# Emitting each q and v projection one unit further ahead in a state-space stage

## The chip, the core and the metric

The kernel runs on one core of one Trainium2 chip. The metric is the device time of one execution in microseconds (us), the median over several executions. The five engines are TensorE (PE, with its weight loads shown as PEld), VectorE (DVE), ScalarE (ACT), GpSimd (POOL) and SyncE (SP, here a queue for transfers).

## What is computed

The reference is one layer of a hybrid trunk on 1024 tokens of width 1024. Only its first third is touched by the change:

```
proj = x @ w_in[i]
q, k, v, u = jnp.split(proj, [ATTN_WIDTH, 2 * ATTN_WIDTH, 3 * ATTN_WIDTH], axis=-1)
...
a_out = _diff_attention(q, k, v, lam, lam_init, subln_g[i])
s_out = _s5_mixer(u, ssm_a_re[i], ssm_a_im[i], ssm_log_dt[i], ssm_b_re[i], ssm_b_im[i],
                  ssm_c_re[i], ssm_c_im[i], ssm_d[i], w_glu[i], b_glu[i])
mix = jnp.concatenate([a_out, s_out], axis=-1) @ w_out[i]
h = _layernorm(alpha * x + mix, ln1_g[i], ln1_b[i])
moe = _hier_moe(h.reshape(b_ * s_, d_), ...).reshape(b_, s_, d_)
x = _layernorm(alpha * h + moe, ln2_g[i], ln2_b[i])
```

The input projection gives q, k, v (4 heads of 128 columns each) and u (512 columns). The attention reads q, k and v; the state-space mixer, a diagonal complex recurrence over 32 groups of 16 channels, reads u alone. So the projections of q, v and k owe nothing to the recurrence and can be worked beside it. A mixture of 32 experts follows and takes more than half of the time.

## The kernel before

All sixteen column tiles of 128 of the input projection go through `proj(ct)`: 48 matmuls of 128x512 (line 244, `proj`), three passes of split-precision products over 8 row tiles, into a PSUM pair of banks. There are two such pairs, used in turn, so that the projection after next can begin only when the result of this one has been copied out. The weights of a column tile arrive by one transfer into a single buffer of the area `misc` (line 191) and are split into a high and a low part, half by half, by a cast on ACT and a subtraction on DVE (tiles `wa` and `wb`, lines 174 and 155). Tiles 12 to 15 are u and come first. Tiles 0 to 3 are q (`proj_q`, copied out by ACT at line 668 into `qr`). Tiles 8 to 11 are v (`proj_v`: copied by ACT at line 678, transposed by PE at line 683, copied again by ACT at line 684). Tiles 4 to 7 are k (`proj_k`: two casts on ACT, lines 692 and 693, and two subtractions on DVE, all four reading the PSUM pair).

The state-space mixer goes through eight units of four channel groups. `ssm_prepare(u)` makes the parameters of unit u, mostly on POOL: a tile X that PE multiplies and transposes (`pk`, `pw`, lines 570 and 571), the convolution kernel `Ks`, to which DVE adds a diagonal `Dd` that a small transfer brings (line 577), eight transfers that spread it into `Tm` (line 582), and the phase tables. `ssm_unit(u)` is a chain: PE (`pz`, line 606), DVE (three products and a sum), four scans on DVE (line 616), two copies on ACT (lines 619 and 620), three products on DVE that give `H`, PE (`py`, line 627 from `Tm`, line 628 from `H`), and a gelu on ACT and DVE (lines 632 and 634). Its tiles are shared from unit to unit. After every second unit PE transposes the result (`zt`, line 660) and ACT copies it (line 661).

`ssm_pair(c4, fill)` emits two units; for unit u it emits the parameters of unit u+1, then the chain of unit u, then `fill(u)`, which is one projection. Four projections of k follow all units, and then the attention, whose first scores are `s` at line 780.

The order of emission is not the order of the queues. A scheduler of the framework reorders the instructions by priorities that come from the order of emission, and gives out buffers as it goes. Each engine then works through its own queue strictly in order, and an instruction that waits holds up all that stands behind it. So what a move in the code does must be read from the queues.

Of the kernel before, what the change touches and what calls it, by code (L numbers as in the profile page):

```python
# [114 lines left out]
def tile_kernel(ctx: ExitStack, tc: tile.TileContext, I: dict, out: bass.AP, dbg=None):  # L115
# [15 lines left out]
    def bank(name, which=0):  # L131

        if which == 1:
            turn[0] ^= 1
            which = 2 + turn[0]
        return psum.tile([P, 512], F32, tag=f"bank{which}", name=name, bufs=1 if which else 2)
# [4 lines left out]
    def dump(name, t):  # L141
        if name in dbg:
            SP.dma_start(dbg[name], t)
# [13 lines left out]
    def mul(out_, a, b, eng=V):  # L157
        eng.tensor_tensor(out=out_, in0=a, in1=b, op=ALU.mult)  # L158

    def add(out_, a, b, eng=V):  # L160
        return eng.tensor_tensor(out=out_, in0=a, in1=b, op=ALU.add)  # L161
# [70 lines left out]
    def proj(ct):  # L232

        first = ct == 12
        if first:
            turn_x(0)
        wt = split_w(ct)
        o = bank2(f"proj{ct}")

        def products(kt, halves):  # L240
            h_, l_ = xh[kt // 2][:, kt % 2, :], xl[kt // 2][:, kt % 2, :]
            for n, (w_, x_) in enumerate(((0, h_), (0, l_), (1, h_))):
                for hs in halves:
                    PE.matmul(o[:, hs], wt[kt // 4][:, w_, kt % 4, :], x_[:, hs],  # L244
                              start=(kt == 0 and n == 0), stop=(kt == KT - 1 and n == 2))

        for halves in ((HALVES[0:1], HALVES[1:2]) if first else (HALVES,)):
            if first and halves == HALVES[1:2]:
                turn_x(1)
                sl.put(*xraw)  # L250
            for kt in range(KT):
                products(kt, halves)
        return o
# [284 lines left out]
    def wk(name, shape, bufs=1):  # L538
        return areas[where[name]].get(name, shape[1:], bufs=bufs, parts=shape[0])
# [7 lines left out]
    def ssm_prepare(u):  # L547

        gs = slice(4 * u, 4 * u + 4)

        def power(pw, first):
            return pw[:, first:first + 8, gs].rearrange("p k g -> p g k").unsqueeze(3).broadcast_to([P, 4, 8, 16])

        def per_c(b_):
            return b_[:, gs, :].unsqueeze(2).broadcast_to([P, 4, 8, 16])

        def combine(o, a1, b1_, a2, b2_, op, eng, name):
            t_ = wk(name, [P, 4, 8, 16])
            mul(o, a1, b1_, eng)
            mul(t_, a2, b2_, eng)  # L560
            op(o, o, t_, eng)

        X = wk("X", [P, 4, 8, 16])
        combine(X, per_c(BB1), power(LR, 0), per_c(BB2), power(LI, 0), add, G, "tb")

        pk = bank(f"pk{u}")
        pw = bank(f"pw{u}", 1)
        for g in range(4):
            Xg = X[:, g, :, :].rearrange("p k c -> p (k c)")
            PE.matmul(pk[:, 16 * g:16 * g + 16], Xg, CA[:, 4 * u + g, :], start=True, stop=True)  # L570
            PE.transpose(pw[:, g * P:(g + 1) * P], Xg, ident)
        Wm = wk(f"Wm{u % 2}", [P, 4, P])
        S.copy(Wm, pw)
        Ks = wk("Ks", [P, 64], 2)
        S.copy(Ks, pk[:, 0:64])
        Dd = wk("Dd", [16, 4, 16])
        SP.dma_start(Dd, I["ssm_d"][0, gs].partition_broadcast(16))
        mul(Dd, Dd, ident[0:16, 0:16].unsqueeze(1).broadcast_to([16, 4, 16]))
        add(Ks[0:16, :], Ks[0:16, :], Dd.rearrange("p g c -> p (g c)"))
        Tm = Tms[u % 2]  # L580
        for t_ in range(8):
            SP.dma_start(Tm[16 * (7 - t_):P, t_].rearrange("p g c -> p (g c)"), Ks[0:16 * (t_ + 1), :])
        M = wk(f"M{u % 2}", [P, 4, 8, 16])
        combine(M, per_c(CA), power(LR, 1), per_c(CB), power(LI, 1), add, G, "tb")

        def low(a_):
            return a_[:, gs, :].unsqueeze(2).broadcast_to([P, 4, 8, 16])

        def high(a_):
            return a_[:, gs, :].unsqueeze(3).broadcast_to([P, 4, 8, 16])  # L590


        C = wk(f"C{u % 2}", [P, 4, 8, 16])
        Sn = wk(f"Sn{u % 2}", [P, 4, 8, 16])
        combine(C, low(cL), high(cH), low(sL), high(sH), sub, G, "tb")
        combine(Sn, low(sL), high(cH), low(cL), high(sH), add, V, "tv")
        return Wm, Tm, M, C.rearrange("p g a b -> p g (a b)"), Sn.rearrange("p g a b -> p g (a b)")
# [42 lines left out]
    def ssm_pair(c4, fill):  # L640
        z2 = wk("z2", [P, 8, P])
        if c4 % 2 == 0:
            zT[c4 // 2] = sl.get([P, 2, T], F32, f"zT{c4 // 2}")
        UT = UTs[c4 // 2][:, c4 % 2, :, :]
        for u in (2 * c4, 2 * c4 + 1):
            if u + 1 < NG // 4:
                made[u + 1] = ssm_prepare(u + 1)
            if u + 2 == NG // 4:
                spp.close()
                areas[0].close()  # L650
            ssm_unit(u, UT, z2, made.pop(u))
            if u + 2 == NG // 4:
                areas[1].close()
            fill(u)
        if c4 % 2 == 1:
            sl.put(UTs.pop(c4 // 2))
        for tq in range(2):
            pz = bank(f"zt{c4}{tq}", tq)
            for t_ in range(4):
                PE.transpose(pz[:, t_ * P:(t_ + 1) * P], z2[:, 4 * tq + t_, :], ident)  # L660
            S.mul(zT[c4 // 2][:, c4 % 2, :].rearrange("p (b t) -> p t b", t=8)[:, 4 * tq:4 * tq + 4, :],
                  pz.rearrange("p (t b) -> p t b", t=4), 0.5)

    def proj_q(h):
        o = proj(h)
        if h % 2 == 0:
            qr[h // 2] = sl.get([P, 2, T], F32, f"qr{h // 2}")
        S.mul(qr[h // 2][:, h % 2, :], o, 0.125)
# [27 lines left out]
        kk[h] = t_  # L696

    fills = [(proj_q, 0), (proj_q, 1), (proj_q, 2), (proj_q, 3), (proj_v, 0), (proj_v, 1), (proj_v, 2), (proj_v, 3)]
    made[0] = ssm_prepare(0)
    for c4 in range(4):  # L700
        ssm_pair(c4, lambda u: fills[u][0](fills[u][1]))
    dump("zT0", zT[0])
    dump("zT1", zT[1])
    for a_ in areas[2:5]:
# [182 lines left out]
    fills = {}  # L887
# [729 lines left out]
```

## Time and profile before

| what | value |
| --- | --- |
| median of 3 runs | 1185.71 us (1184.47 to 1189.87) |
| time of the profiled execution | 1182.18 us |
| span of the profiled execution, first to last instruction | 1180.4 us |
| mean granted clock of TensorE | 0.968 of full speed |
| busy share of PE, DVE, ACT, POOL | 92%, 82%, 60%, 30% |

Rows of the profile give a start in us from the beginning of the span, a length in us, the engine, the line and operation, the tile written and the tiles read, and how often it repeats. A bracket at a row's end is the idle time of the engine just before it and what ended that. The granted clock has two levels, 1.0 (2.4 GHz) and 0.5 (1.2 GHz). Names without a number mean any of their kind: `ssm` stands for any tile of the state-space areas.

### The profile page before, as it was taken

The numbers are of one execution on the slowest core, as the hardware profiler recorded it, in microseconds if no ns is written. First come the engines' busy times: TensorE is split into PE (matmuls) and PEld (weight loads), VectorE is DVE, ScalarE is ACT, GpSimd is POOL, SyncE is SP. The second block draws the span as 40 slices with busy tenths as digits, with TensorE's granted clock in tenths as the row PEclk, the third lists the DMA queues.
The fourth block names the chain that finished last, engine by engine and source line by source line (L and its number), as shares of the span: only waits on it lengthen the run. The fifth ranks groups of instructions, "written<-read, shape, count | busy, mean of one in ns | idle before, by whom it ended". The sixth has DMA issues, their size and how long they took to land.

```text
span 1180.4 us, 15229 instructions
## 1 busy us (share of the span) xinstructions
PE 1081.9 (92%) x5345; PEld 902.0 (76%) x5345; DVE 970.2 (82%) x1430; ACT 711.6 (60%) x960; POOL 359.0 (30%) x297
## 2 busy tenths in 40 slices
PE   6979999896779899995999999999999999999983
PEld 4867887686668788884888888888888888888852
DVE  4898666657878874565999999999999999999955
ACT  3312333445656743213888888888888888888832
POOL 1087464422442643341212122122122122121122
PEclk9989999998999999995999999999999999999997
DMA  8531111211181454545699999999999999999582
GB/s 208 138 99 43 55 46 46 59 30 42 32 325 36 159 210 136 196 178 200 238 361 378 383 369 399 383 385 396 381 374 376 377 370 386 395 386 386 172 208 108
DMA packets 90622, 278.90 MB, mean 236 GB/s; under 512 B 29404, under 2 KB 49900, under 8 KB 66096
## 3 DMA queue, kind: packets, MB, share of 16 engines
q1 hardware_dynamic: 78016, 252.78, 57.1%
q0 software_dynamic: 11520, 24.83, 7.7%
q8 instruction: 43, 0.70, 0.2%
q10 hardware_dynamic: 1008, 0.30, 0.1%
q14 instruction: 35, 0.29, 0.1%
HBM read 254.12 MB, written 34.60 MB: 245 GB/s over the span
## 4 chain that ended last, share of the span: by engine, by line
PE 74%; DVE 13%; ACT 5%; DMA 3%; issue 3%; SPq 1%; POOL 1%; ACTq 0%; DVEq 0%; POOLq 0%
PE g L1246 15%; PE u L1246 14%; PE y L1237 14%; PE proj L244 8%; PE mix L1077 7%; PE xT L1207 3%; DMA misc<-in_w_in_dram 2%; ACT p L783 2%; PE glu L733 2%; PE po L818 1%; PE hT L1219 1%; PE x L1449 1%; PE pl L1099 1%; DVE ssmt L158 1%; DVE ssm L158 1%
## 5 line engine op out<-in xcount | busy, mean ns | idle before, releaser
L1146 POOL DMA_INDIRECT moe_dram<-yo,idx x30 | 52.1, 1738 | 425.9 <-DVE yo L164 425.9
L244 PE MATMUL proj<-xh,wa 128*128 128x512 f32 x256 | 75.9, 403 | 1.7 <-ACT ssm L678 1.6
L244 PE MATMUL proj<-xh,wb 128*128 128x512 f32 x256 | 73.9, 400 | 1.6 <-ACT ssm L678 1.6
L1077 PE MATMUL mix<-woh,mx 128*128 128x512 f32 x256 | 74.3, 401 | 0.7 <-ACT p L783 0.7
L1141 POOL DMA_INDIRECT gx<-h_dram,idx x32 | 60.2, 1881 | 22.5 <-DVE WT L161 13.1
L783 ACT ACTIVATE p<-s,nm 128x1024 f32<-128x1024 f32 (+7 forms) x64 | 47.3, 745 | 26.8 <-DVE nm L798 17.0
L244 PEld LDWEIGHTS proj<-xh,wa 128*128 128x128 f32 x256 | 48.6, 193 | 11.8 <-ACT ssm L678 1.8
L244 PEld LDWEIGHTS proj<-xh,wb 128*128 128x128 f32 x256 | 48.0, 191 | 11.4 <-ACT ssm L678 1.8
L1077 PEld LDWEIGHTS mix<-woh,mx 128*128 128x128 f32 x256 | 48.1, 191 | 10.5 <-ACT p L783 1.0
L1253 ACT ACTIVATE yo<-y,WT 128x1024 f32<-128x1024 f32 (+1 forms) x33 | 36.0, 1091 | 24.4 <-PE y L1237 24.4
L780 PE MATMUL s<-kk,qh 128*128 128x512 f32 (+3 forms) x96 | 38.0, 399 | 12.5 <-ACT p L783 12.2
L818 PE MATMUL po<-vv,half 128*128 128x128 f32 x288 | 43.4, 294 | 6.7 <-ACT half L815 6.6
L818 PEld LDWEIGHTS po<-vv,half 128*128 128x128 f32 x288 | 39.2, 205 | 9.9 <-ACT half L815 8.7
L1207 PEld LDWEIGHTS xT<-ident,gx 128*128 128x128 f32 x256 | 36.2, 208 | 9.9 <-DMA gx<-h_dram,idx 5.8
L1207 PE MATMUL xT<-ident,gx 128*128 128x128 f32 x256 | 36.9, 287 | 7.0 <-DMA gx<-h_dram,idx 5.6
L155 DVE TENSOR_TENSOR xe<-xT,xe 128x1024 fp32r<-128x1024 f32 (+1 forms) x33 | 39.2, 1189 | 4.3 <-ACT xe L174 4.3
L244 PE MATMUL proj<-xl,wa 128*128 128x512 f32 x128 | 42.6, 404 | 0.0
L164 DVE SCALAR_TENSOR_TENSOR yo<-gx,first,yo 128x1024 f32<-128x1024 f32 (+1 forms) x33 | 41.3, 1252 | 1.5
L1077 PE MATMUL mix<-wol,mx 128*128 128x512 f32 x128 | 42.2, 398 | 0.0
L244 PE MATMUL proj<-xl,wb 128*128 128x512 f32 x128 | 41.4, 399 | 0.0
L174 ACT CAST xe<-xT 128x1024 fp32r<-128x1024 f32 (+1 forms) x33 | 32.3, 979 | 13.6 <-PE xT L1207 13.6
L164 DVE SCALAR_TENSOR_TENSOR p<-p,rho 128x1024 f32<-128x1024 f32 (+7 forms) x32 | 36.2, 1135 | 1.0 <-DMA moe_dram<-zero 0.3
(864 smaller groups left out, 3546.7 us busy)
## 6 DMA issues: line engine op xcount, KB each, us to landing
misc<-in_w_in_dram SPq DMA_DIRECT2D x16, 512.0 KB, 3.9
moe_dram<-zero SPq DMA_DIRECT2D x4, 2048.0 KB, 13.2
xr<-in_x_dram SPq DMA_DIRECT2D x8, 512.0 KB, 8.5
wo_raw<-in_w_out_dram SPq DMA_DIRECT2D x4, 1024.0 KB, 4.8
xa<-in_x_dram SPq DMA_DIRECT2D x8, 512.0 KB, 3.5
h_dram<-xa SPq DMA_DIRECT2D x8, 512.0 KB, 3.2
mo<-moe_dram SPq DMA_DIRECT2D x8, 512.0 KB, 6.0
mo<-moe_dram POOLq DMA_DIRECT2D x8, 512.0 KB, 13.1
```

Source lines behind the costliest of these rows:

```text
L155: eng.tensor_tensor(out=out_, in0=a, in1=b, op=ALU.subtract)
L164: return V.scalar_tensor_tensor(out=out_, in0=a, scalar=s, in1=b, op0=op0, op1=op1)
L244: PE.matmul(o[:, hs], wt[kt // 4][:, w_, kt % 4, :], x_[:, hs], start=(kt == 0 and n == 0), stop=(kt == KT - 1 and n == 2))
L780: PE.matmul(s_[:, c0:c0 + w], qd[0][:, c, tk], kk[h][:, c, c0:c0 + w], start=True, stop=False)
L783: S.activation(p_[:, c, 0:n], s_[:, 0:n], AF.Exp, bias=nm[:, c:c + 1], accum_out=L[:, j, c:c + 1])
L818: PE.matmul(po[:, j * P:(j + 1) * P], aT[:, k, :], vv[k // 4][:, k % 4, h * P:(h + 1) * P], start=(k == 0), stop=(k == i))
L1077: PE.matmul(o[-(hs.start > 0)][:, hs], mx[:, m_, kt, :], (woh, wol)[w_][kt // 2][:, kt % 2, hs], start=(kt == 0 and n == 0), stop=(kt == K ...
L1141: return G.indirect_dma_start(out=dst, out_offset=None, in_=h_dram[:, :], in_offset=bass.IndirectOffsetOnAxis(ap=ix, axis=0), bounds_check ...
L1146: G.indirect_dma_start(out=moe_dram[:, :], out_offset=bass.IndirectOffsetOnAxis(ap=ix, axis=0), in_=src, in_offset=None, bounds_check=2 * ...
L1207: PE.transpose(b_[:, kt * P:(kt + 1) * P], rows(g_, kt), ident)
L1237: PE.matmul(y[h_], hid[e][:, x_, kt, :], w_[:, k, HALVES[h_]], start=(kt == 0 and n == 0), stop=(kt == 3 and n == 2))
L1246: PE.matmul(o, xT[e][:, x_, kt, :], w_[:, k, :], start=(kt == 0 and n == 0), stop=(kt == KT - 1 and n == 2))
```

## The change

The list of projections is shifted by one: `proj_q(0)` is emitted directly behind the parameters of unit 0, and unit u is followed by the projection that used to follow unit u+1. Behind unit 7 nothing is emitted any more. No instruction is added, removed or resized.

```
     fills = [(proj_q, 0), (proj_q, 1), (proj_q, 2), (proj_q, 3), (proj_v, 0), (proj_v, 1), (proj_v, 2), (proj_v, 3)]
+    fills.append((lambda _: None, 0))
     made[0] = ssm_prepare(0)
+    proj_q(0)
     for c4 in range(4):
-        ssm_pair(c4, lambda u: fills[u][0](fills[u][1]))
+        ssm_pair(c4, lambda u: fills[u + 1][0](fills[u + 1][1]))
```

The queues show it at three places. In their rows a name ends with the unit or column tile and a serial number: `pk1` belongs to the parameters of unit 1, `proj0` to the first tile of q, `proj1` to the second.

First, PE where the units begin. Before, 29 of the 48 matmuls of `proj0` and `pz0` stand ahead of `pk1`:

```order
L244 MATMUL proj0_833<-xl1_84,wa_66 128x512 x2
L244 MATMUL proj0_833<-xh1_80,wa_66 128x512
L606 MATMUL pz0_797<-UT0_282,ssm10_719 128x128 x4
L244 MATMUL proj0_833<-xh1_80,wa_66 128x512
L244 MATMUL proj0_833<-xh2_81,wa_66 128x512 x2
L244 MATMUL proj0_833<-xl2_85,wa_66 128x512 x2
L244 MATMUL proj0_833<-xh2_81,wa_66 128x512
L570 MATMUL pk1_765<-ssmp0_292,ssm00_718 128x16
L571 MATMUL pw1_766<-ident_72,ssm00_718 128x128
```

After, on the same engine at the end of `proj0`:

```order
L244 MATMUL proj0_766<-xh3_82,wa_66 128x512 x2
L570 MATMUL pk1_821<-ssmp0_292,ssm00_718 128x16
L571 MATMUL pw1_822<-ident_72,ssm00_718 128x128
...
L606 MATMUL pz0_853<-UT0_282,ssm10_719 128x128 x4
L244 MATMUL proj1_889<-xh0_79,wb_67 128x512 x2
L244 MATMUL proj1_889<-xl0_83,wb_67 128x512 x2
L244 MATMUL proj1_889<-xh0_79,wb_67 128x512 x3
L627 MATMUL py0_871<-ssm20_720,UT0_282 128x8x16
L244 MATMUL proj1_889<-xh0_79,wb_67 128x512
```

All 48 matmuls of `proj0` now stand ahead of `pk1`, `pz0` stands behind it, and the first product of `py0` comes seven matmuls into `proj1`.

Second, DVE at the same place, as a piece of the difference. The rows `ssm_722<-pz` begin the chain of unit 0, the row with `ident` is the product that reads the diagonal `Dd` of unit 1, and the rows `wa` split the weights of `proj2`:

```order
 L158 TENSOR_TENSOR ssm_718<-ssmp_293 128x512
-L158 TENSOR_TENSOR ssm_722<-pz_797,ssm_719 128x512
-L158 TENSOR_TENSOR ssm_722<-pz_797,ssm_719 64x512 x2
-L155 TENSOR_TENSOR wa<-misc_68,wa 128x512
+L155 TENSOR_TENSOR wa<-misc_68,wa 128x512 x2
+L158 TENSOR_TENSOR ssm_718<-ssm_718,ident 16x64
+L161 TENSOR_TENSOR ssm_718<-ssm_718 16x64
+L158 TENSOR_TENSOR ssm_722<-pz_853,ssm_719 128x512
+L158 TENSOR_TENSOR ssm_722<-pz_853,ssm_719 64x512 x2
 L161 TENSOR_TENSOR ssm_722<-ssm_722 128x512
 L616 SCALAR_TENSOR_TENSOR ssm_720<-mag,ssm_722 128x128 x4
```

The product with the diagonal, which stood behind the scans of unit 0, now stands ahead of the whole chain of unit 0.

Third, PE where the recurrence ends beside the projections of k (`proj5`, `proj6`, `proj7` are the second to fourth). Before, `py6` stands inside `proj5`:

```order
L244 MATMUL proj5_1878<-xh2_81,wb_67 128x512
L628 MATMUL py6_1606<-ssm10_719,ssm20_720 128x8x16
L627 MATMUL py6_1606<-ssm20_720,UT2_584 128x8x16
...
L244 MATMUL proj5_1878<-xh2_81,wb_67 128x512
L244 MATMUL proj5_1878<-xh3_82,wb_67 128x512 x2
L244 MATMUL proj5_1878<-xl3_86,wb_67 128x512 x2
L244 MATMUL proj5_1878<-xh3_82,wb_67 128x512 x4
```

After, it stands four matmuls ahead of the end of `proj6`:

```order
L244 MATMUL proj6_1947<-xh3_82,wa_66 128x512 x4
L628 MATMUL py6_1673<-ssm10_719,ssm20_720 128x8x16
L627 MATMUL py6_1673<-ssm20_720,UT2_584 128x8x16
...
L244 MATMUL proj6_1947<-xl3_86,wa_66 128x512 x2
L244 MATMUL proj6_1947<-xh3_82,wa_66 128x512 x2
L244 MATMUL proj7_2006<-xh0_79,wb_67 128x512 x2
```

And ACT after, behind `py6`; the casts `kk1` read the PSUM pair of `proj5`, which is the pair that `proj7` takes next:

```order
L632 ACTIVATE ssm40_722<-py6_1673 128x512
L692 CAST kk1_1927<-proj5_1878 64x1024
L693 CAST kk1_1927<-proj5_1878 64x1024
L634 ACTIVATE ssm40_722<-ssm40_722 128x512
L619 COPY ssm40_722<-ssm20_720 64x512
```

Before, the casts `kk1` stood behind `py6` too, but 13 matmuls of `proj5` and all 48 of `proj6` lay on PE between `py6` and `proj7`; now 4 do. In the same way `py7` stood behind the first 11 matmuls of `proj7`, 37 ahead of its end; now it stands behind 40, 8 ahead of the end, and the casts of `proj6` (`kk2`) stand behind it on ACT.

## Rows read from the trace of the kernel before

**Rows 1.** Windows: length, busy PE, PEld, DVE, ACT, POOL, granted clock, DMA share, GB/s.

```profile
126.00:199.00 73.00, 72.59 (x396) 61.84 (x395) 44.74 (x70) 25.45 (x41) 36.12 (x29) 1.00 0.17 44
```

**Rows 2.** Timeline of PE, its rows with idle time, 77 to 126 us.

```profile
85.28 0.61 PE L570 MATMUL pk<-ssmp,ssm 128*128 128x16 f32 x2 [7.65 <-POOL ssm L161]
...
99.37 0.49 PE L628 MATMUL py<-ssm,ssm 128*128 128x128 f32 x2 [1.26 <-DVE ssm L155]
...
119.58 0.49 PE L628 MATMUL py<-ssm,ssm 128*128 128x128 f32 x2 [2.88 <-DVE ssm L155]
```

**Rows 3.** Timeline of PE, its rows with idle time, 126 to 264 us.

```profile
199.41 0.66 PE L683 MATMUL v<-ident,ssm 128*128 128x128 f32 x4 [0.68 <-ACT vv L684]
...
201.66 0.73 PE L244 MATMUL proj<-xh,wa 128*128 128x512 f32 x2 [1.59 <-ACT ssm L678]
...
218.40 0.49 PE L627 MATMUL py<-ssm,UT 128*128 128x128 f32 x2 [0.88 <-ACT zT L661]
...
219.31 1.16 PE L606 MATMUL pz<-UT,ssm 128*128 128x128 f32 x8 [0.43 <-ACT ssm L575]
...
221.85 0.66 PE L683 MATMUL v<-ident,ssm 128*128 128x128 f32 x4 [0.94 <-ACT vv L684]
...
224.10 1.07 PE L244 MATMUL proj<-xh,wb 128*128 128x512 f32 x2 [1.59 <-ACT ssm L678]
...
234.98 0.49 PE L628 MATMUL py<-ssm,ssm 128*128 128x128 f32 x2 [0.79 <-DVE ssm L155]
```

**Rows 4.** Windows, columns as in rows 1, where the clock is lower.

```profile
90.00:91.00 1.00, 1.00 (x4) 0.71 (x4) 0.97 (x2) 0.00 (x0) 1.00 (x1) 0.50 0.45 131
224.00:228.00 4.00, 3.90 (x10) 3.09 (x11) 3.94 (x4) 0.04 (x1) 1.86 (x1) 0.57 0.10 21
```

**Rows 5.** The chain that ended last: start, length, what.

```profile
103.32 1.75 DMA ssm<-in_ssm_d_dram
...
121.41 7.51 PE proj L244 x33
```

**Rows 6.** Timelines: PE behind the first hole, SP's transfers of units 0 and 1.

```profile
87.43 1.63 PE L244 MATMUL proj<-xh,wa 128*128 128x512 f32 x3
...
90.28 3.09 SPq L582 DMA_DIRECT2D ssm<-ssm  x5
93.42 0.59 SPq L577 DMA_DIRECT2D ssm<-in_ssm_d_dram  x1
```

**Rows 7.** Timeline of DVE: the scans of units 0, 1 and 6.

```profile
90.13 5.12 DVE L616 TENSOR_TENSOR_SCAN ssm<-mag,ssm 128x128 f32<-128x128 f32 x4
...
113.48 1.37 DVE L616 TENSOR_TENSOR_SCAN ssm<-mag,ssm 128x128 f32<-128x128 f32 x4
...
225.91 5.68 DVE L616 TENSOR_TENSOR_SCAN ssm<-mag,ssm 128x128 f32<-128x128 f32 x4
```

**Rows 8.** Timelines of ACT and DVE: how `proj6` is copied out.

```profile
257.67 0.60 ACT L632 ACTIVATE ssm<-py 128x512 f32<-128x512 f32 x1
...
259.18 1.01 ACT L693 CAST kk<-proj 64x1024 fp32r<-64x1024 f32 x1
...
260.22 2.46 DVE L155 TENSOR_TENSOR kk<-proj,kk 64x1024 fp32r<-64x1024 f32 x2 [1.23 <-ACT kk L693]
```

**Rows 9.** Timelines of PE, DVE and ACT where the attention begins.

```profile
263.98 0.39 PE L780 MATMUL s<-kk,qh 128*128 128x512 f32 x1
...
265.29 1.22 DVE L798 TENSOR_REDUCE nm<-s 128x1 f32<-128x1024 f32 x1
...
268.04 1.08 ACT L783 ACTIVATE p<-s,nm 128x1024 f32<-128x1024 f32 x1
...
269.26 0.79 PE L780 MATMUL s<-kk,qh 128*128 128x512 f32 x1 [3.33 <-ACT p L783]
```

**Rows 10.** Timelines of DVE and PE in unit 2: `H`, and its first reader.

```profile
144.86 0.67 DVE L155 TENSOR_TENSOR ssm<-ssm,ssm 128x508 f32<-128x508 f32 x1
...
147.69 0.38 PE L628 MATMUL py<-ssm,ssm 128*128 128x128 f32 x2
```

## The prediction

> **What bounds the kernel now.** The table ahead says that PE is busy for 92% of the span, so I looked first for the stretches in which it is not. The windows show the middle of the state-space stage as full: 72.59 of 73.00 us at a granted clock of 1.00 [rows 1]. There the reader is to see that a move can save nothing: the projections, 33 matmuls in 7.51 us or 0.228 us each, stand one behind the other on the chain that ended last [rows 5]. PE's own timeline then shows where it stands still: in the first units, for POOL's tile X and for DVE's `H` [rows 2], and in units 5 and 6, for ACT, which copies v and the transposed results out [rows 3]. Last I read where the projections of k end and the attention begins [rows 8, 9], since the work that no longer lies beside unit 7 is missing there. The mixture of experts behind it is the same, instruction for instruction, so I let what is won or lost by then pass to the end one to one. The sum is made against the profiled 1182.18 us, which lies 3.5 us under the median; I put its result on the median.
>
> **The change part by part.** Nothing is added or taken away; all terms are waits and what the clock does behind them. Gains carry a plus.
>
> *The first hole.* PE stands still for 7.65 us ahead of `pk1`, until POOL has made X of unit 1 [rows 2]. POOL's queue is as it was, so X comes at the same time. Ahead of `pk1` there are now 48 matmuls of `proj0` in place of 29: 19 more at 0.228 us are 4.3. `pz0`, 8 passes, 1.16 us in unit 6 [rows 3] and about 0.9 of it unhidden, goes behind. The hole becomes about 4.2 us: **+3.4**.
>
> *Unit 0.* After 85.28, `pk1` and `pw1` take 2.15 us, as before [rows 2, 6]. Then come `pz0` and seven matmuls of `proj1`. The clock is at 0.50 until about 91 [rows 4], and I keep that: `pz0` counts 1.8 us (between 1.16 and twice that), four matmuls count double, three single, and PE reaches the first product of `py0` at about 91.75. That product reads `Tm0`. SP's five last copies of it end their issue at 93.37, the last begun some 0.6 before [rows 6], and a small transfer lands 1.75 us after its start [rows 5]: about 94.6. PE waits some 2.85 us, where it waited 1.26 before [rows 2]: **-1.6**. On DVE the product with unit 1's diagonal stands ahead of unit 0's chain now. Its transfer begins at 93.42 [rows 6] and lands at about 95.2, so DVE, free from about 88, waits some 7 us with the whole chain of unit 0 queued behind it. POOL waits for that chain too, so its scans run beside no POOL work, in 1.4 us rather than 5.1 [rows 7]. I count `H0` at about 104.2 and PE there at 104.75. This half microsecond is the thinnest margin of the front: I take no wait, with 1.3 as the other bound.
>
> *Unit 1.* PE waited 2.88 us for `H1` [rows 2]. By the same count `H1` is ready at about 118.5, and PE, with a whole projection more in front of it, comes at about 121: **+2.9**, and nothing if DVE is 2.9 us later than I count. On SP's queue the weight load of `proj3` now stands ahead of unit 1's copies of `Tm`; the buffer that it waits for is free by about 88, so it holds them up by nothing. The front gives +4.7.
>
> *Units 2 to 4* are full before and after: nothing.
>
> *Units 5 and 6.* Between 199 and 224 PE waits 0.68, 1.59, 0.88, 0.43, 0.94 and 1.59 us, 6.1 in all, each time for ACT [rows 3]. Behind the last of them the clock is 0.57 for 4 us [rows 4], which loses 1.7. Together 7.8. In the new order the copies and transposes of each v come a unit earlier, away from the copies of `zt`, and 14 matmuls of `proj5` lie beside these. The margins that I count at the six places are 0.2 to 1 us, so I take one of them as lost: **+6.8** of 0 to 7.8.
>
> *`py6`.* It waited 0.79 us for `H6` [rows 3], behind scans that took 5.68 us beside POOL, against 1.37 with POOL idle [rows 7]. They still run beside POOL; I count 1.5: **-0.7**.
>
> *`proj7`.* This is the new wait. `proj7` needs the PSUM pair of `proj5`, which `kk1` frees: two casts on ACT, queued behind the gelu of `py6`, then two subtractions on DVE. The same sequence for `proj6` starts with the gelu at 257.67, has its casts done at 260.19 and its subtractions at 262.68 [rows 8]: 5.0 us. Before, a projection and a quarter hid it. Now four matmuls, 0.9 us, lie between: **-4.1**, or nothing if ACT finds room for the casts before the gelu.
>
> *The clock behind it.* In the trace PE's clock fell in the 7.65 us hole and was still 0.50 at 90 to 91 [rows 2, 4]. If a stop of 4.1 us does the same, 5.7 us pass at half speed: **-2.9**, else 0. I take the fall.
>
> *The attention's start.* The first scores began with no wait at 263.98. The next ones came 5.28 us later, 3.33 of it idle, behind a reduction on DVE and an exponential on ACT [rows 9]. Now `py7` is 8 matmuls, 1.8 us, ahead of the end of `proj7`, and `kk2` follows its gelu with the same 5.0: the first scores start 3.2 us after the end of `proj7` instead of at it. Behind them come 1.3 us of scores, 1.22 of reduction, 1.08 of exponential and some 0.3 between: 7.1 us instead of 5.28 until the second scores: **-1.8**.
>
> Sum: 4.7 + 6.8 - 0.7 - 4.1 - 2.9 - 1.8 = **+2.0**: 1180.2 us profiled, 1183.7 on the median. A difference under 0.5%, 5.9 us, I hold to be one that measuring this kernel can't tell from none.
>
> **The rivals.** *k's copy-out holds nobody* (faster). The casts of `kk1` begin before `py6` is done, or the wait lies in a pause that PE has anyway. Then the last three losses, 8.8 us, fall away: 1174.9. For it speaks that no `proj` matmul in the trace waits for DVE's `kk`; against it that only four matmuls are left as cover where the sequence takes 5.0 us [rows 8] and the queue holds the casts behind the gelu. The Trainium skill, "Perfetto Trace Analysis", section "Matmuls", says that independent groups of matmuls should go to different PSUM banks in turn, so that one group's copy-out overlaps the next group's matmuls. By that rule alone the two pairs used in turn would suffice and this rival's time would come; the trace agrees as long as a whole projection lies between, and no row before shows fewer.
>
> *The recurrence becomes the bound* (slower). With DVE's chain starting later and its scans beside POOL in every unit, each `py` of units 2 to 5 and 7 would come late. A contended set of scans costs 5.68 - 1.37 = 4.3 us more [rows 7]; in unit 2 `H` was ready at 145.53 and PE there at 147.69, 2.2 us of room [rows 10]. So 2.1 us each, 10.5 in all: 2.0 - 10.5 = -8.5, or 1194.2. It decides, that is passes 0.5%, from 7.9 us of such waits, 1.6 a unit. Against it: one projection more stands ahead of each chain, and PE waited for no `H` between 126 and 199 [rows 1, 3]. The Trainium skill, "SBUF — State Buffer", section "Who interferes with whom", has it that a DVE instruction with two operands in SBUF contends with a GpSimd instruction reading SBUF; the scans' two durations agree with it.
>
> *The waits at 199 to 224 stay.* ACT is simply short there and the shift only exchanges one wait for the next: the change does not do at that place what its order says. Then 6.8 falls away: 1190.5, which is no measurable change.
>
> **How the numbers follow.** My sum 0.48, with a range of its own from 1180 to 1188 (one microsecond more at the middle and no fall of the clock; or a wait at `py0` and half of the middle's gain). k's copy-out hidden 0.20, the recurrence 0.17, the waits that stay 0.15. Faster by more than 0.5% means under 1179.8: the first rival and a little of my own case, 0.22. Slower means over 1191.6: the second rival, 0.17. The rest, 0.61, is the same. The range reaches to the first rival's 1174.9 and, above, past the third's 1190.5: 1174.5 to 1192.
>
> **What would show it.** In the changed kernel: a hole ahead of `pk1` of 4 us, not 7.65; DVE idle for some 7 us on the transfer of `ssm_d` near 88; PE's wait at `py1` gone and one of about 3 at `py0`; next to no waits of PE for ACT where v is copied; a new idle time of about 4 us at the first matmul of the last projection, ended by DVE's `kk`, with a clock of 0.50 behind it; and the first scores late by 3 us. Wrong would be above all: no idle time at that last projection (the first rival), or PE idle on DVE's `H` in unit after unit (the second). A wait at `py0` for `H0` as well would show that I counted the front half a microsecond too well.

## The result, and the profile after

The changed kernel takes 1197.31 us (median of 5, 1197.14 to 1199.52) where the kernel before takes 1185.71 (1183.66 to 1189.87): the ratio is 1.0107, with a 95% interval of 1.0091 to 1.0123. It is slower by 1.1%, over the 0.5% that counts, and outside the range that I gave (1174.5 to 1192).

The two profiled executions lie 17.3 us apart, 1182.18 and 1199.52, the two medians 11.6. The profile of before is one of its kernel's quick executions. A second profile of the same kernel, taken later as a control (`e11_again`, 1187.19 us, median 1184.66), stands 12.3 us under the profile of after, close to the difference of the medians, and I take the differences against it.

First, PE's timeline of the changed kernel, its rows with idle time of over half a microsecond up to the attention's second scores, which answer to [rows 2, 3, 9]. The bracket is the idle time ahead and what ended it.

```profile
84.56 0.40 PE L570 MATMUL pk<-ssmp,ssm 128*128 128x16 f32 x2 [3.81 <-POOL ssm L161]
...
94.13 0.77 PE L627 MATMUL py<-ssm,UT 128*128 128x128 f32 x2 [4.06 <-DMA ssm<-ssm]
...
206.03 0.63 PE L683 MATMUL v<-ident,ssm 128*128 128x128 f32 x4 [1.56 <-DVE misc L164]
...
212.64 1.12 PE L683 MATMUL v<-ident,ssm 128*128 128x128 f32 x4 [2.54 <-ACT vv L684]
...
214.81 0.80 PE L628 MATMUL py<-ssm,ssm 128*128 128x128 f32 x2 [1.06 <-DVE ssm L155]
...
244.14 0.49 PE L627 MATMUL py<-ssm,UT 128*128 128x128 f32 x2 [0.62 <-ACT vv L684]
...
252.56 0.73 PE L244 MATMUL proj<-xh,wb 128*128 128x512 f32 x2 [4.22 <-DVE kk L155]
...
272.15 0.76 PE L782 MATMUL s<-kk,qh 128*128 128x512 f32 x1 [5.21 <-issue]
...
277.19 0.80 PE L782 MATMUL s<-kk,qh 128*128 128x512 f32 x1 [1.29 <-ACT p L785]
```

The reader is to see three places: the hole ahead of `pk1` is halved, as it was to be (7.65 in [rows 2]); the middle still waits at 206 to 215, once for ACT and twice for DVE; and there are two new stops, 4.22 us ahead of the last projection, ended by DVE's `kk`, and 5.21 us ahead of the first scores.

Now windows of the same kernel (length, busy time of PE, PEld, DVE, ACT, POOL with counts, granted clock, DMA share, GB/s), cut at the first scores (272.15) and at the first product of the output projection (429.98):

```profile
69.00:126.00 57.00, 49.13 (x240) 40.93 (x240) 45.54 (x68) 14.00 (x25) 33.73 (x27) 0.91 0.19 55
126.00:199.00 73.00, 72.74 (x400) 62.19 (x400) 43.66 (x66) 25.63 (x41) 38.47 (x30) 1.00 0.16 43
199.00:240.00 41.00, 35.83 (x180) 30.24 (x179) 23.91 (x31) 14.54 (x21) 18.78 (x15) 0.92 0.19 47
240.00:272.15 32.15, 22.09 (x103) 17.41 (x101) 17.32 (x26) 11.31 (x15) 8.01 (x8) 0.92 0.11 25
272.15:429.98 157.83, 129.84 (x742) 111.92 (x742) 129.73 (x248) 97.98 (x204) 63.61 (x49) 0.88 0.35 121
```

And those of the control, cut at the same two places of the program (265.18 and 419.12):

```profile
69.00:126.00 57.00, 47.77 (x233) 40.02 (x233) 49.75 (x71) 14.04 (x25) 42.88 (x30) 0.88 0.20 55
126.00:199.00 73.00, 72.87 (x397) 62.29 (x396) 43.56 (x67) 24.56 (x39) 35.20 (x29) 1.00 0.16 44
199.00:240.00 41.00, 34.17 (x180) 27.96 (x179) 28.09 (x34) 17.88 (x26) 18.98 (x16) 0.96 0.24 58
240.00:265.18 25.18, 25.18 (x124) 21.05 (x122) 13.66 (x19) 10.30 (x14) 6.82 (x6) 1.00 0.09 19
265.18:419.12 153.94, 123.59 (x743) 107.04 (x742) 122.77 (x245) 97.91 (x204) 61.83 (x46) 0.93 0.36 121
```

The control's first and second scores, on PE:

```profile
265.18 0.39 PE L780 MATMUL s<-kk,qh 128*128 128x512 f32 x1
...
270.45 0.80 PE L780 MATMUL s<-kk,qh 128*128 128x512 f32 x1 [3.33 <-ACT p L783]
```

Idle time is the length less PE's busy time; what the lower clock costs is PE's busy time times (1 - clock). The front cost 9.2 us idle and 5.7 of clock in the control, 7.9 and 4.4 after: a gain of 2.6. The stretch from 199 to 240: 6.8 and 1.4 against 5.2 and 2.9, a gain of 0.1. From 240 to the first scores the control has no idle time and a full clock; after, 10.1 us are idle and 1.8 lost by the clock. That one stretch, 11.9 us, takes back what the change wins and is about as large as the whole loss. From the first scores to the output projection after takes 3.9 us more. Behind it the two kernels differ by 1.4 us (769.5 and 768.1 to the end). The control comes 1.9 us later to `pk0`, ahead of all that the change touches (70.43 against 68.54), so that up to the attention the change costs 1.9 us more than a comparison at fixed times shows.

### The profile page after: what moved, and what is told of

Read it like the earlier page. It is cut to its first block, busy times and chain, and to the rows that moved or that the text cites. A ratio compares the mean times of both kernels' runs of the same rounds, so it can differ in the third digit from the quotient of the medians.

```text
span 1197.7 us, 15223 instructions
## 1 busy us (share of the span) xinstructions
PE 1096.2 (92%) x5345; PEld 913.1 (76%) x5345; DVE 971.1 (81%) x1430; ACT 710.2 (59%) x960; POOL 354.7 (30%) x297
## 4 chain that ended last, share of the span: by engine, by line
PE 72%; DVE 14%; DMA 4%; ACT 4%; issue 3%; SPq 2%; POOL 0%; ACTq 0%; DVEq 0%; POOLq 0%
PE g L1248 15%; PE u L1248 14%; PE y L1239 14%; PE mix L1079 7%; PE proj L244 6%; PE xT L1209 3%; DMA misc<-in_w_in_dram 2%; PE po L820 2%; PE glu L735 2%; DVE p L164 1%; ACT p L785 1%; PE hT L1221 1%; PE x L1451 1%; PE pl L1101 1%; DVE ssm L158 1%
## 5 line engine op out<-in xcount | busy, mean ns | idle before, releaser
L820 PEld LDWEIGHTS po<-vv,half 128*128 128x128 f32 x288 | 40.9, 214 | 11.7 <-ACT half L817 10.5
L164 DVE SCALAR_TENSOR_TENSOR p<-p,rho 128x1024 f32<-128x1024 f32 (+7 forms) x32 | 40.6, 1272 | 1.1 <-DMA moe_dram<-zero 0.3
```

Source lines behind the costliest of these rows:

```text
L164: return V.scalar_tensor_tensor(out=out_, in0=a, scalar=s, in1=b, op0=op0, op1=op1)
L820: PE.matmul(po[:, j * P:(j + 1) * P], aT[:, k, :], vv[k // 4][:, k % 4, h * P:(h + 1) * P], start=(k == 0), stop=(k == i))
```

## The experiments

Sixteen runs: one repeats the kernel before, the others are told in groups. Their medians and ratios come first; the three times behind them are read in each run's profile: where the row of the last product of unit 7 (`py7`) begins, the first scores, and the first product of the output projection.

| kernel | median us | ratio to before (95% interval) | py7 | scores | output proj. |
| --- | --- | --- | --- | --- | --- |
| e11_again (before) | 1184.66 | 0.9999 (0.9985 to 1.0013) | 256.5 | 265.2 | 419.1 |
| after | 1197.31 | 1.0107 (1.0091 to 1.0123) | 264.7 | 272.2 | 430.0 |
| e1_front | 1191.56 | 1.0049 (1.0030 to 1.0069) | 258.1 | 265.6 | 422.5 |
| e2_late | 1186.84 | 1.0007 (0.9991 to 1.0023) | 259.7 | 267.2 | 422.8 |
| e3_diag | 1192.58 | 1.0068 (1.0046 to 1.0089) | 266.0 | 273.4 | 429.2 |
| e4_slot | 1189.51 | 1.0032 (1.0017 to 1.0047) | 257.2 | 264.7 | 419.2 |
| e5_spread | 1196.91 | 1.0094 (1.0069 to 1.0119) | 264.1 | 271.6 | 429.3 |
| e6_ask | 1196.95 | 1.0094 (1.0069 to 1.0119) | 264.6 | 272.0 | 429.1 |
| e7_combo | 1186.12 | 1.0014 (0.9995 to 1.0033) | 255.5 | 263.0 | 417.4 |
| e8_bslot | 1192.08 | 1.0065 (1.0042 to 1.0088) | 254.6 | 262.1 | 422.8 |
| e9_fill | 1194.83 | 1.0088 (1.0072 to 1.0103) | 263.6 | 271.0 | 426.7 |
| e10_combofill | 1184.41 | 0.9999 (0.9983 to 1.0014) | 259.3 | 266.8 | 417.5 |
| e12_afterpy7 | 1189.68 | 1.0033 (1.0017 to 1.0048) | 256.0 | 265.6 | 423.0 |
| e13_queries | 1198.45 | 1.0119 (1.0096 to 1.0142) | 262.9 | 267.7 | 427.8 |
| e14_comboq | 1187.55 | 1.0022 (1.0002 to 1.0041) | 256.1 | 261.0 | 418.3 |
| e15_comboqd | 1189.21 | 1.0039 (1.0023 to 1.0054) | 261.2 | 266.0 | 424.0 |
| e16_beforeq | 1188.05 | 1.0030 (1.0012 to 1.0047) | 257.8 | 266.4 | 419.2 |

Behind the output projection's first product, 765 to 770 us follow in every profile, so what is read there reaches the end.

**Parts of the change.** `e1_front` keeps the early projection of q and leaves a gap behind unit 0; `e2_late` starts the shift at unit 3.

```
# e1_front, on the changed kernel
+    fills = [(proj_q, 0), (lambda _: None, 0), (proj_q, 1), (proj_q, 2), (proj_q, 3), (proj_v, 0), ...]
# e2_late, on the kernel before; q3_v0 emits both
+    fills = [(proj_q, 0), (proj_q, 1), (proj_q, 2), (q3_v0, 0), (proj_v, 1), (proj_v, 2), (proj_v, 3), (lambda _: None, 0)]
```

> q's first projection is emitted early as in the change, but no projection follows unit 0, and from unit 1 on all stand as before, so v's last one follows unit 7 again. Theory A (the loss is made where the recurrence ends, since no projection lies beside unit 7): the front's gain stays and the tail is that of before, 1180 to 1184 us. Theory B (the loss is made in front and middle, by DVE waiting for the transfer of the diagonal, 6.5 us in unit 0): DVE still waits there and the time is 1188 to 1192. Theory C (the half clock in the attention comes or not by chance): 1190 to 1197 as often as 1185.

> Units 0 to 2 as before; two projections (q's last and v's first) follow unit 3, and from there all stand one unit ahead, nothing behind unit 7. Theory A: the tail of the changed kernel without its front, a new idle time of about 4 us ahead of k's last projection and first scores 5 us late, 1194 to 1199 us. Theory B: near before, 1184 to 1188, since the first unit's wait for the diagonal is absent. Theory C: anywhere between.

Measured: `e1_front` is 0.5% slower, `e2_late` the same as before. Theory A, as I had put it, falls: a tail without a projection beside unit 7 does not by itself cost 8 to 13 us. In `e2_late` PE has no idle time ahead of k's last projection (the only stop from 240 on is 7.04 us ahead of the first scores), and it is the change as a whole, not its late half, that makes that stop. The casts of `kk1` stand right behind the gelu of `py6` there too, but PE has 25 matmuls of `proj6` left behind `py6`, where the changed kernel has four.

The same run shows the middle. From 199 to 240 PE stands still for 1.5 us in it, at full clock, where the control loses 8.2 us and the changed kernel 8.1; the product with the diagonal stands behind the scans there and does not wait (a window of `e2_late`, then DVE):

```profile
199.00:240.00 41.00, 39.46 (x208) 32.65 (x206) 29.93 (x37) 16.93 (x25) 21.52 (x18) 1.00 0.28 59
```

```profile
203.80 4.09 DVE L616 TENSOR_TENSOR_SCAN ssm<-mag,ssm 128x128 f32<-128x128 f32 x4
...
210.41 1.08 DVE L158 TENSOR_TENSOR ssm<-ssm,ident 16x64 f32<-16x64 f32 x1
```

So the gain that I had counted in the middle exists: it comes when only the late units are shifted, and not in the changed kernel. `e2_late` loses it again by the stop of 7.04 us ahead of the first scores and, in this profile, by 3.8 us more than the control in the front, where its emitted order is that of the kernel before.

**Where k's second tile is copied to.** The scheduler's buffers, 25 of them, go round in the order in which they come free. Read from the order of allocation, `kk1` takes the one that holds the parameters of unit 6, which PE reads until `py6` is done. `e4_slot` takes an earlier one; `e8_bslot` does that in the kernel before.

```
-        t_ = sl.get([P, 2, T], F32R, f"kk{h}")
+        t_ = sl.get([P, 2, T], F32R, f"kk{h}") if h != 1 else kk1
...
     proj_k(0)
+    kk1 = sl.get([P, 2, T], F32R, "kk1")
     qd = {0: queries(0)}
```

> The changed kernel, with the copy of k's second tile placed in a buffer that is free before unit 6 ends (it took one that holds unit 6's parameters), and the tiles behind it shifted by one buffer. Theory A: PE's 4.2 us ahead of k's last projection and the half clock behind it (1.8) go, 1190 to 1193 us, with the late first scores unchanged. If the casts stand behind the gelu of unit 6 for the order of the queue alone and not for the buffer: no change, 1197. Theory B and C: 1195 to 1199.

> The kernel before, with k's second tile in the early buffer alone. PE has no wait there, since a projection and a quarter lies between: no change by that, 1184 to 1187. Were it faster by over 5 us, the buffer would be a gain of its own and not a cure for the change.

In the changed kernel, ACT's casts of `kk1` and DVE's subtractions come behind the gelu of `py6`, 14 us after PE has finished `proj5`, which they read (at 233.9):

```profile
247.50 0.60 ACT L632 ACTIVATE ssm<-py 128x512 f32<-128x512 f32 x1 [3.42 <-PE py L628]
...
249.00 1.01 ACT L693 CAST kk<-proj 64x1024 fp32r<-64x1024 f32 x1
...
250.04 2.46 DVE L155 TENSOR_TENSOR kk<-proj,kk 64x1024 fp32r<-64x1024 f32 x2 [1.22 <-ACT kk L693]
```

In `e4_slot` they are done long before it (ACT and DVE, then PE at the first scores):

```profile
232.04 1.00 ACT L692 CAST kk<-proj 64x1024 fp32r<-64x1024 f32 x1
...
235.94 2.46 DVE L155 TENSOR_TENSOR kk<-proj,kk 64x1024 fp32r<-64x1024 f32 x2
...
245.17 0.60 ACT L632 ACTIVATE ssm<-py 128x512 f32<-128x512 f32 x1 [7.18 <-PE py L628]
...
264.66 0.76 PE L782 MATMUL s<-kk,qh 128*128 128x512 f32 x1 [7.05 <-issue]
```

The casts move 16 us ahead, the idle time ahead of k's last projection is gone, `py7` comes 7.5 us sooner (257.2 against 264.7), and the median falls by 7.8 us, two thirds of the loss. That is a little more than the 4 to 7 that I expected. From 240 to `py7` the changed kernel has 4.85 us of idle time and 1.4 lost by the clock, and `e4_slot` neither, which is 6.2; some 2 us more come from the middle, where PE's first stop falls from 1.56 to 0.26 us. The edit changes where buffers lie and not the order in which the work is emitted; ACT's order follows from it. So the stop needs both: the late buffer, and `py6` so near the end of `proj6` (in `e2_late`, with the same buffer, the work behind `py6` hides the copy). The edit is not that one wait alone, though: behind it a dozen of PE's rows ahead of the first scores and some 120 from there on stand in another order. `e8_bslot` missed: it is 0.65% slower although its `py7` and first scores come 2 and 3 us sooner than in the control. Its stretch from the scores to the output projection takes 160.7 us (153.9 in the control); the scheduler has reordered some 75 of PE's rows, two thirds of them from the first scores on. Which of these costs it was not tried.

**The wait for the diagonal.** `e3_diag` loads the diagonals two units ahead.

```
+    def load_d(u):
+        if u < NG // 4:
+            Dds[u] = wk("Dd", [16, 4, 16], 4)
+            SP.dma_start(Dds[u], I["ssm_d"][0, 4 * u:4 * u + 4].partition_broadcast(16))
+    load_d(0)
+    load_d(1)
     def ssm_prepare(u):
+        load_d(u + 2)
...
-        SP.dma_start(Dd, I["ssm_d"][0, gs].partition_broadcast(16))
+        Dd = Dds[u]
```

> The changed kernel, with the diagonals loaded two units ahead into four buffers, so that DVE does not wait for them. Theory B: the idle times of PE at 206 to 215 us (5.2 us and the half clock behind them) shrink and the time falls by 5 to 8 us to 1189 to 1192. Theory A: the tail stays as it is, 1194 to 1198; the waits in the middle may go, and most of what they give is then waited for at the end.

DVE does wait in the changed kernel, 6.53 us in unit 0 and again in the middle, and ACT's copies of v are late (DVE, then ACT behind the recurrence's copies, with what held each):

```profile
94.78 0.57 DVE L158 TENSOR_TENSOR ssm<-ssm,ident 16x64 f32<-16x64 f32 x1 [6.53 <-DMA ssm<-in_ssm_d_dram]
...
203.22 0.69 DVE L158 TENSOR_TENSOR ssm<-ssm,ident 16x64 f32<-16x64 f32 x1 [3.00 <-DMA ssm<-in_ssm_d_dram]
...
210.73 0.62 ACT L619 COPY ssm<-ssm 64x512 f32<-64x512 f32 x1 [5.05 <-DVE ssm L616]
...
212.00 0.59 ACT L684 COPY vv<-v 128x512 f32<-128x512 f32 x1
```

In `e3_diag` DVE's wait in the middle is gone, and so is the first of PE's three stops there (1.56); the others stay (2.35 and 1.19), and the first scores come no sooner (273.4). In unit 0 the wait only shrinks, from 6.53 to 4.14 us: on SP's queue the transfer still stands behind the spread of u. The median is 4.7 us under that of after, with executions from 1188.5 to 1197.1: not the mechanism of theory B, and not explained by its profile (1195.8). With the tail mended, `e15_comboqd` adds the same to `e14_comboq` and is not faster:

> e14_comboq with the diagonals loaded two units ahead as in e3_diag. If DVE's wait for the diagonal costs anything once the tail is mended, 1 to 3 us less than e14_comboq; if not, the same within 1 us.

It took 1189.21 us against 1187.55. That does not settle what the wait costs, since the edit takes away the one in the middle and lengthens the one in unit 0 (3.93 us in `e14_comboq`). DVE there, first in `e3_diag`, then in `e15_comboqd`, and PE in the latter, which waits for `H0`:

```profile
96.36 0.42 DVE L158 TENSOR_TENSOR ssm<-ssm,ident 16x64 f32<-16x64 f32 x1 [4.14 <-DMA ssm<-in_ssm_d_dram]
```

```profile
96.83 1.00 DVE L158 TENSOR_TENSOR ssm<-ssm,ident 16x64 f32<-16x64 f32 x1 [6.14 <-DMA ssm<-in_ssm_d_dram]
...
106.95 0.80 PE L643 MATMUL py<-ssm,ssm 128*128 128x128 f32 x2 [3.58 <-DVE ssm L155]
```

So `py7` comes 5 us later than in `e14_comboq`, and what the wait for the diagonal costs stays open.

**The first unit's transfers.** SP spreads the last tile of u, eight transfers, ahead of five of the copies of `Tm` of unit 0. `e5_spread` emits these behind unit 0; `e7_combo` is that with `e4_slot`.

```
+        def spread():
+            for s_ in range(8):
...
+        if c4 == 3:
+            return spread
+        spread()
...
             ssm_unit(u, UT, z2, made.pop(u))
+            if u == 0:
+                spread3()
```

> The changed kernel, with the eight transfers that spread the last tile of u emitted behind unit 0 instead of ahead of it, so that the copies of Tm of unit 0 do not stand behind them on SP's queue. If PE's 4.06 us at the first product of unit 0 are those transfers: the idle time falls to 0 to 1 us, the half clock behind it goes, and proj's end comes 3 to 6 us earlier; the time falls to 1191 to 1194 if the tail is bound by PE, and stays at 1196 to 1198 if the recurrence's last unit sets the first scores anyway.

> The changed kernel with both: k's second tile in the early buffer (e4_slot) and the transfers of u behind unit 0 (e5_spread). If PE bounds the way to the attention: the gains add, 1183 to 1187. If the chain of the recurrence bounds it (unit 7's product, its gelu, the copy-out of k's third tile): first scores as in e4_slot, at about 264, and 1188 to 1190.

SP's queue after, and PE in `e5_spread` at the first product of unit 0:

```profile
84.86 4.80 SPq L269 DMA_DIRECT2D UT<-u_dram  x8
89.70 3.08 SPq L582 DMA_DIRECT2D ssm<-ssm  x5
```

```profile
91.19 0.77 PE L632 MATMUL py<-ssm,UT 128*128 128x128 f32 x2 [0.53 <-issue]
```

The wait goes from 4.06 to 0.53 us, so it was those transfers; the time hardly follows (1196.91). The stops of 4.23 and 5.21 us behind are the same, and the profile came 1.7 us later to `pk0` (70.23), so that `py7` is only 0.6 us sooner; why the median does not fall by the rest is not shown. With the buffer mended, `e7_combo` is 3.4 us under `e4_slot` by the medians and 2.1 by the ratios, whose intervals overlap, and equal to the kernel before within its interval. That fits a way there that PE bounds; it does not prove it.

**The clock at the attention's start.** PE's clock after, in the windows from the stop ahead of the scores on, and that of the control behind its own 3.33 us:

```profile
270.00:288.00 18.00, 12.43 (x43) 10.53 (x44) 13.57 (x22) 9.77 (x18) 2.83 (x4) 0.53 0.23 52
297.00:305.00 8.00, 7.02 (x33) 6.04 (x31) 5.11 (x12) 3.76 (x10) 0.91 (x2) 0.57 0.42 98
```

```profile
270.00:281.00 11.00, 8.42 (x30) 7.37 (x31) 6.99 (x16) 4.62 (x12) 0.00 (x0) 0.53 0.01 1
294.00:298.00 4.00, 3.57 (x15) 3.19 (x16) 2.54 (x5) 1.73 (x5) 0.00 (x0) 0.57 0.17 45
```

`e9_fill`, `e10_combofill` (on `e7_combo`) and `e12_afterpy7` (on `e7_combo`, held back until `py7` is done) add work that nobody reads in that stop: 20 and 28 matmuls, and 44 transposes.

```
     proj_k(3)
+    idle = psum.tile([P, 512], F32, tag=f"bank{2 + (turn[0] ^ 1)}", name="fill", bufs=1)
+    for j in range(20):
+        PE.matmul(idle, wa[:, 0, 0, j % 4, :], xh[j % 4][:, 0, 0:512], start=True, stop=True)
```

> The changed kernel with 20 matmuls of 128x512 added behind k's last projection, whose result nobody reads; in PE's queue they stand between the last projection and the first scores, where PE stands still for 5.2 us. Theory D (the loss in the attention is the clock, which falls in that pause and stays at half through three rounds of scores): the first scores start at the same time but at full clock, the first stretch of half clock shrinks from 17 us to some 10, and the time falls by 3 to 5 us, to 1192 to 1194. If the attention is bound by its softmax there and not by PE's clock: no change, 1196 to 1198.

> e7_combo with 28 such added matmuls in the pause of over 7 us ahead of the first scores. Theory D: 1181 to 1184, under the kernel before. Otherwise as e7_combo, 1185 to 1188.

> e7_combo, and in the pause of 7 us behind the last product of unit 7, 44 transposes of 128x128 that nobody reads and that can begin only behind that product (a copy of a part of it on ACT, 0.3 us, releases them). In e10_combofill 17 of the added matmuls stood ahead of unit 7's product and put it off by 3.8 us, so that the fuller clock was paid for by a later start. Theory D: first scores at 263 to 264 as in e7_combo, the attention as short as in e10_combofill (151 us), 1181 to 1183, under the kernel before by 0.2 to 0.3%. If the attention's length is chance or order and not the clock at its start: 1185 to 1187.

In `e9_fill` the stop is nearly gone (PE, the added matmuls, the first scores, the second) and the first slow stretch is 11 us long instead of 18:

```profile
265.64 4.71 PE L855 MATMUL fill<-xh,wa 128*128 128x512 f32 x20
...
271.02 0.47 PE L782 MATMUL s<-kk,qh 128*128 128x512 f32 x1 [0.68 <-issue]
...
276.80 0.79 PE L782 MATMUL s<-kk,qh 128*128 128x512 f32 x1 [3.75 <-ACT p L785]
```

```profile
276.00:287.00 11.00, 8.07 (x30) 7.02 (x31) 7.01 (x16) 4.62 (x12) 0.00 (x0) 0.54 0.01 1
```

The second scores, which waited 1.29 us for ACT's exponential in the changed kernel, wait 3.75 for it now. From the scores to the output projection it takes 155.6 us (157.8 after), and the time falls by 2.5 us, a little less than the 3 to 5 that I expected; the intervals of the two ratios overlap. `e10_combofill` is 1.7 us under `e7_combo`, within their intervals: 17 of the 28 matmuls stand ahead of `py7` and put it off by 3.8 us, and the attention, 150.7 us long, gives that back. `e12_afterpy7` missed: its transposes wait 2.75 us for the copy on ACT that releases them, put off the first scores to 265.6, and the attention takes 157.4 us. So the clock in the stop is worth some 2 to 4 us of that stretch (155.6 against 157.8, and 150.7 against 154.4 in `e7_combo`), of which the medians keep 2.5 and 1.7. That is about what the stretch differs by between two profiles of one program (below), and not the 7 by which the clock's cost differs in the windows of after and control from the first scores on (129.84 x 0.12 against 123.59 x 0.07).

**The queries asked for.** `e6_ask` moves the copies of the queries of head 2 from the sixth to the ninth unit of the attention; `e13_queries`, `e14_comboq` and `e16_beforeq` move those of head 1 behind k's third projection, in the kernels after, `e7_combo` and before.

```
# e6_ask, on the changed kernel
-ASK, GLU, WO = (6, 12), (15, 16, 1, 20, 21, 1), (22, 24, 26, 30)
+ASK, GLU, WO = (9, 12), (15, 16, 1, 20, 21, 1), (22, 24, 26, 30)
# e13_queries, on the changed kernel
-    qd[1] = queries(1)
     proj_k(2)
+    qd[1] = queries(1)
     proj_k(3)
```

> The changed kernel, with the copies of the queries of head 2 asked for at the ninth unit of the attention instead of the sixth. If the third stretch of half clock (297 to 305 us after, absent in the kernel before) comes from POOL's subtractions of these copies beside DVE's scaling: the pause of 2.25 us ahead of it and the stretch go, 3 to 5 us less, 1192 to 1194. If the attention only suffers from its late and slow start: no change, 1196 to 1198.

> The changed kernel, with the copies of the queries of head 1 emitted behind k's third projection instead of ahead of it. On ACT the casts of k's third tile then stand ahead of unit 7's gelu and of the two query casts (2.12 us) that held them up, and take a buffer that is free with unit 7's product. Theory D: the first scores come 2.5 us sooner behind that product (4.6 us instead of 7.1), the 5.2 us pause halves, and with less half clock behind it the time falls by 3 to 5 us, to 1192 to 1194; the 4.2 us ahead of the last projection of k stay. If the softmax of head 1 then waits for its queries: no gain, 1196 to 1198.

> e7_combo with the same move of the queries of head 1. Theory D: first scores at 260 to 261 instead of 263, 1181 to 1184, under the kernel before. If the attention takes back what it gets earlier: 1185 to 1187.

> The kernel before with the move of the queries of head 1 alone: its first scores have no wait, so no change, 1184 to 1187. A gain here of over 3 us would mean that the move pays by itself.

`e6_ask` changed nothing that can be measured: its pauses and slow stretches are elsewhere, not fewer. `e13_queries` does at the scores what was expected. After, ACT and DVE behind unit 7:

```profile
264.90 2.12 ACT L765 CAST qh<-qr 64x1024 fp32r<-64x1024 f32 x2 [5.71 <-PE py L627]
267.05 0.60 ACT L632 ACTIVATE ssm<-py 128x512 f32<-128x512 f32 x1
...
268.55 1.01 ACT L693 CAST kk<-proj 64x1024 fp32r<-64x1024 f32 x1
...
269.59 2.46 DVE L155 TENSOR_TENSOR kk<-proj,kk 64x1024 fp32r<-64x1024 f32 x2 [1.22 <-ACT kk L693]
```

In `e13_queries`, ACT there, and PE's first scores and output projection:

```profile
263.07 1.01 ACT L692 CAST kk<-proj 64x1024 fp32r<-64x1024 f32 x1 [5.71 <-PE py L627]
...
267.69 0.47 PE L782 MATMUL s<-kk,qh 128*128 128x512 f32 x1 [2.58 <-issue]
...
427.81 0.73 PE L1079 MATMUL mix<-woh,mx 128*128 128x512 f32 x2 [2.22 <-ACT p L785]
```

The two query casts of 2.12 us were what I had left out: with them gone the first scores come 4.8 us behind the start of `py7`'s last row instead of 7.5. But the median does not fall (1198.45), and the stretch from the scores to the output projection is 160.1 us. `e14_comboq` repeats it: scores 2 us sooner than in `e7_combo`, the attention 3 us longer, no gain. `e16_beforeq` loses 0.3%. In these two kernels an earlier first score is given back in the attention; what takes it back was not tried.

**The control.**

> The kernel before once more, with a new profile, to see how far its attention varies from execution to execution: from the first scores to the first product of the output projection 151 us in the profile shown, 154 to 161 in all changed kernels. If its order fixes that, 150 to 152 again; if it is chance, up to 156.

The same program took 153.9 us from scores to output projection, 2.8 more than in the first profile, with a slow stretch at 294 to 298 that the first profile does not have. So some 3 us of this length differ between two executions of one program.

## Why the prediction was wrong

*Units 5 and 6* are the step that failed first: the forecast took 6.8 us there, and the stretch from 199 to 240 gave 0.1. PE still stands still for 5.2 us between 206 and 215, in other places than before (1.56 and 1.06 us for DVE, 2.54 for ACT), and 2.9 us go to the clock. That is my rival "the waits at 199 to 224 stay" in its outcome, but not in its reason: ACT is not simply short, since in `e2_late`, with v one unit earlier too, the stretch loses 1.5 us instead of 8.2. I had counted margins of 0.2 to 1 us at six places, and took five of the six as held. I had also left out DVE's wait of 3.00 us for the diagonal. The stop of 1.56 us is gone without it (`e3_diag`), but nearly gone with it too (0.26 in `e4_slot`, where DVE waits 3.06). The 2.54 us are a wait for an ACT copy of v that is queued behind copies waiting for DVE's scans, as the trace shows; why they come too late for PE in the changed kernel and not in `e2_late` stays open.

*The attention* is the second step, and by size the larger: 9.1 us were lost from the end of the last projection to the output projection, where 1.8 were counted. The first scores came 5.2 us behind the last projection instead of 3.2, for the two query casts, which I had left out. From the first to the second scores it took 5.0 us, nearly as in the control (5.3), and not the 3.9 that the sum allowed. The rest of the attention, which I held to be fixed, took some 4 us more; some 2 of these may be the clock (`e9_fill`), and 3 are no more than the control varies by.

*The front* gave 2.6 us against the control (3.6 against the profile on which the sum was made) instead of 4.7. *The first hole* was right: 3.8 us against 4.2 worked out. *Unit 0* was too good: PE waited 4.06, not 2.85, and its clock stayed at half from 93 to 99; DVE's wait was the 7 us foreseen, at 6.53. *Unit 1*: the wait went, as said.

*`py6`, `proj7` and the clock behind it* held. The wait at `proj7` was 4.22 us against 4.1, `py6` waited 0.62 us (for ACT's copy of v, not for `H6`) where 1.5 were counted, and the slow clock cost about 1.7 us, not 2.9. From 240 to the end of the last projection that is 6.6 us, where the three terms come to 7.7; and `e4_slot`, which takes the stop away, gives back 7.8 in the median, with some 2 of its `py7` from the middle. The reason I had only half: the casts wait for a buffer of unit 6 and not only behind its gelu.

So the losses up to the last projection were foreseen in full; the gain in the middle that was to pay for them did not come, and the attention lost more than was counted. Against the control's profile the sum is 14.3 us too good (+2.0 forecast, -12.3 measured): 6.7 of it in the middle, some 7 from the end of the last projection to the output projection, 2.1 in the front and 1.4 behind the attention, less 1.1 at the tail and 1.9 for the control's later start.

Where does the loss appear? Most of it is there when unit 7 ends. `py7` is at 256.5 in the control and at 264.7 after, 8.2 us later; of the 10.9 us by which the output projection starts later, that is three quarters. From the last row of `py7` to the output projection the seventeen profiles of the table take 158 to 168 us, fourteen of them 161 to 166. That spread is nearly as wide as the whole loss, so `py7` alone does not give the time: `e8_bslot` has the earliest `py7` of all and is slower than before.

Of the rivals, "k's copy-out holds nobody" is excluded by the 4.22 us. By the Trainium skill, "Perfetto Trace Analysis", section "Matmuls", two pairs of banks in turn should have let the copy-out overlap; the trace shows that turning banks does not help by itself where the copy's destination is not free. "The recurrence becomes the bound" did not come true: PE waited for `H` 0.26 us in unit 3 and 1.06 in unit 5, and in units 2, 4, 6 and 7 not at all, where 10.5 in all were counted.

Open stay the attention's own differences: `e8_bslot` loses 0.65% with an earlier `py7`, `e1_front` 0.5% with `py7` 1.6 us later than in the control. Both have other orders in the attention's queues, and no run here pins such an order down. Nor was the late spread of u tried on the kernel before, so how much of `e7_combo` is a mend of the change and how much a gain of its own is not known.

No version beats the kernel before: the best, `e10_combofill` (0.9999), `e2_late` (1.0007) and `e7_combo` (1.0014), only make up for the change.

## What to carry to other kernels

Price the gains of a move as strictly as its losses: a wait that is to vanish is gone only if nothing else ends there later in the new order, and six margins of under a microsecond are a rival and not a term of the sum. Work that is moved away from the end of a serial chain leaves that end bare: ask there which buffer, not only which engine, each copy-out waits for, and how much work is left to hide it. When an edit is to take a wait away, look in its trace whether it did, at every place, before its time is read. Take a second profile of the kernel before you explain a difference of under 5 us: here two profiles of one program lay 5.0 us apart.

## What the runs showed of the hardware that was not expected

PE's granted clock, once at 0.5 in the stop ahead of the first scores, stayed there for some 17 us, with two further pauses of 1.29 and 2.13 us among the rounds of scores; with the stop filled (`e9_fill`) the clock was full until the next pause. Yet of the 7 us of clock that separate after from the control there, filling the stop gave back some 2. From the first scores to the output projection PE was busy for 4.5 us less (125.3 against 129.8) and idle for 2.3 us more: half of what it did faster it waited longer for, at first for ACT's exponential (3.75 us in place of 1.29).
